# Products over 640 tokens on TensorE: column segments of 512 and 128 in place of 320 and 320

## The chip, the cores and the metric

The kernel runs on one core of a Trainium2 chip. The metric is the device time of one execution in microseconds, from the first to the last instruction with what lies around them; the median of several runs counts. The core has five engines with their own instruction queues: TensorE (PE; its weight loads are listed apart as PEld), VectorE (DVE), ScalarE (ACT), GpSimd (POOL) and SyncE (SP, which here issues most DMAs).

## The reference, cut to what matters

One layer of a hybrid diffusion backbone for 640 tokens (128 context tokens and 512 latent ones) of width 1024, in float32:

```
z = h @ w_in + b_in                      # 1024 -> 3584, h = modulated LayerNorm of x
u_a, u_b, g_a, g_b = split(z)            # 1024, 512, 1024, 1024 columns
v = gelu(s5_forward(u_a) + s5_backward(u_a))
v = v * sigmoid(v @ w_glu + b_glu)
ya = v @ w_proj_a
yb = pool_mix(u_b, w_pool, pool_scale) @ w_proj_b
x = LN(alpha*x + gate*((sigmoid(g_a)*ya + sigmoid(g_b)*yb) @ w_out + b_out))
x = LN(alpha*x + gate*(square(relu(h2 @ w_mlp1 + b_mlp1)) @ w_mlp2 + b_mlp2))
```

## The kernel before, in words

All float32 products are made of three products of the float32r type: each operand is split into a high part and a low remainder (`split`, lines 320 to 322: a cast on ACT, a subtraction on DVE), and high by high, high by low and low by high are added up in PSUM (`PASS`, line 331). The tokens lie along the columns of the moving operand, the output channels are the 128 columns of the stationary one. A PSUM bank holds 512 float32 columns, so the 640 tokens need two banks (`bank2`, a tile of 128 x 2 x 512) and two matmuls for each pass and each block of 128 input channels. `SEG` (line 31) says which tokens go to which: 0 to 319 into the first bank, 320 to 639 into the second. `mm_k` (lines 333 to 337) issues, for one block of input channels, the three passes, and in each pass the two segments with the same 128x128 weights, so the segments alternate: first segment, second segment, first, second. Each matmul has its own weight load in the trace.

Products that go through `mm_k` with `SEG`, in order of time, with the matmuls of each:

- the input projection `w_in`, 28 products of 48 matmuls: two next to the making of the operand `hk` (`chan`, line 388), six for `u_a` (`ua_evac`, each followed by two calls of `more_in`, which transpose and project on TensorE too), and 20 "fillers" for `u_b` and the gates (`plain`, `halves`), of which 16 are called during the scan, one in four of the scan's steps on DVE, and three are cut into halves between the calls of `out_proj`;
- `pool_map`, four products of 6 matmuls, and `pool_proj`, eight products of 24 matmuls, between calls of `out_proj`;
- `w_glu`, eight products of 48 (line 845, the first two interleaved at line 843), and `w_pa`, eight products of 48 (line 873).

That is 1344 + 24 + 192 + 384 + 384 = 2328 matmuls or 1164 pairs of segments. The two MLP products use `mm_k` with `SEG_MLP` (384 and 256 columns) or other loops (`mlp_first`, line 979; `prod`, line 1048; line 1119) and are not touched.

A finished pair of banks is read in one instruction: `v2(ps)` takes the first 320 columns of each bank as a 128 x 2 x 320 view, and `tv(t)` views the 640 columns in SBUF the same way. ACT reads it with a bias and a function (lines 364, 612, 629, 708, 852), or DVE multiplies it by a gate (lines 718, 874). Weights come in with `wsplit`: a DMA on SP into one of two raw buffers, the split into one of three `wh` buffers. Other TensorE work around these products is plain float32 (lines 489, 503, 557, 597, 600, 237).

Of the kernel before, what the change touches and what calls it, by code (L numbers as in the profile page):

```python
# [13 lines left out]
AF = mybir.ActivationFunctionType  # L14
# [5 lines left out]
NT = 640  # L20
NTT = 5
KT = 8
TC = 8
# [4 lines left out]
FF = 4 * D  # L28
ALPHA = 2.0 ** 0.25
EPS = 1e-6  # L30
SEG = ((0, 320), (320, 320))
SEG_MLP = ((0, 384), (384, 256))


C_BIN, C_BADA, C_BGLU, C_PSC, C_BM1, C_N = 0, 28, 76, 84, 88, 120
# [3 lines left out]
def hybrid_kernel(ctx: ExitStack, tc: tile.TileContext, xin, cc, w_ada0, w_ada, w_in, w_glu, w_pa, w_pool, w_pb,  # L39
                  w_out, w_m1, w_m2, cols, rows, brow, lam, bpk, cpk, ddg, s0, cst, invc, out, nstate):  # L40
    nc = tc.nc
    V, S, T = nc.vector, nc.scalar, nc.tensor
# [29 lines left out]
    def bank2(name="ps"):  # L72
        return pp[0].tile([P, 2, 512], F32, tag="mm", name=nm(name))

    def bank(name="ax"):
        return pp[0].tile([P, 512], F32, tag="ax", bufs=axn[0], name=nm(name))
# [3 lines left out]
    colt = keep.tile([P, C_N], F32, name="colt")  # L80
# [243 lines left out]
    def wsplit(src, n=D, to=None):  # L324
        raw = wp.tile([P, D], F32, tag="wr", bufs=2, name=nm("wr"))
        hl = wp.tile([P, 2, D], F32R, tag="wh", name=nm("wh")) if to is None else to
        dma(raw[:, 0:n], src)
        split(raw[:, 0:n], hl[:, 0, 0:n], hl[:, 1, 0:n])
        return hl
# [3 lines left out]
    def mm_k(ps, hl, xk, k, nk, segs):  # L333
        for i, (wh, xh) in enumerate(PASS):
            for n, (o, ln) in enumerate(segs):
                T.matmul(ps[:, n, 0:ln], hl[:, wh, k * P:(k + 1) * P], xk[:, xh, o:o + ln],  # L336
                         start=(k == 0 and i == 0), stop=(k == nk - 1 and i == 2))

    def mm(hl, xk, segs=SEG):
        ps = bank2()  # L340
        for k in range(len(xk)):
            mm_k(ps, hl, xk[k], k, len(xk), segs)
        return ps

    def v2(ps):
        return ps[:, :, 0:320]

    def tv(t):
        return t.rearrange("p (n c) -> p n c", n=2)

    ud = dp.tile([KT, TC, P, NC], F32, name="ud")
    urd = dp.tile([KT, TC, P, NC], F32, name="urd")
# [8 lines left out]
    def ua_evac(m, ps):  # L361

        uj = half([P, TC, NC], "uj")
        S.activation(uj[:, ::-1, :].rearrange("p j (n c) -> p j n c", n=2),
                     v2(ps).rearrange("p n (c j) -> p j n c", j=TC),
                     AF.Identity, bias=colt[:, C_BIN + m:C_BIN + m + 1])
        dma(ud[m].rearrange("j p c -> p j c"), uj)
        ur = half([P, TC, NC], "ujr")
        S.copy(ur[:, :, 0:CP], uj[:, :, CP - 1::-1])
        S.copy(ur[:, :, CP:NC], uj[:, :, NC - 1:CP - 1:-1])  # L370
        dma(urd[m].rearrange("j p c -> p j c"), ur)
# [43 lines left out]
    for q in range(4):  # L415
# [3 lines left out]
        for hl, pu in zip(hls0, (pu0, pu1)):  # L419
            for kk in (2 * q, 2 * q + 1):  # L420
                mm_k(pu, hl, hx[kk], kk, KT, SEG)
        if q < 2:
            shift_scale(q + 2)
    ang = s5_angles()
    ua_evac(0, pu0)
    ua_evac(1, pu1)
    s5_params(*ang)
    dma(dd, ddg)
# [180 lines left out]
    def plain(m, func, dst):  # L609
        ps = mm(next_w(), hx)  # L610
        g = gt([P, NT], "g")
        S.activation(tv(g), v2(ps), func, bias=colt[:, C_BIN + m:C_BIN + m + 1])  # L612
        dma(dst, g)
# [5 lines left out]
    def halves():  # L619

        while fillers:
            m, func, dst = fillers.pop(0)
            hl, ps = next_w(), bank2()
            for k in range(KT):
                mm_k(ps, hl, hx[k], k, KT, SEG)
                if k == 3:
                    yield
            g = gt([P, NT], "g")
            S.activation(tv(g), v2(ps), func, bias=colt[:, C_BIN + m:C_BIN + m + 1])
            dma(dst, g)  # L630
            yield
# [19 lines left out]
    for m in range(2, 8):  # L651
        ua_evac(m, mm(next_w(), hx))
        more_in(2, 1)
        if m == 3:
            gen_q(0)
        if m in (4, 6):
            gen_t(m // 2 - 2)
            gen_q(m // 2 - 1)
# [43 lines left out]
    def pool_map(gi, p, wph):  # L702
        ph = hslot([P, 2, NT], F32R, "ph")
        split(p, ph[:, 0, :], ph[:, 1, :])
        ps = bank2()
        mm_k(ps, wph[:, :, gi * P:(gi + 1) * P], ph, 0, 1, SEG)
        f = gt([P, NT], "yb")
        S.activation(tv(f), v2(ps), AF.Identity, scale=colt[:, C_PSC + gi:C_PSC + gi + 1])
        yb = hslot([P, 2, NT], F32R, "ybx")
        split(f, yb[:, 0, :], yb[:, 1, :])  # L710
        ybx.append(yb)
# [129 lines left out]
    for k in range(KT):  # L841
        for m in range(2):
            mm_k(gps[m], hls[m], vx[k], k, KT, SEG)
    for m in range(KT):
        ps = gps[m] if m < 2 else mm(wsplit(w_glu[m]), vx)
# [22 lines left out]
    for m in range(KT):  # L868
# [4 lines left out]
        ps = mm(wsplit(w_pa[m]), [gx[:, k] for k in range(KT)])  # L873
# [47 lines left out]
    for t in range(NTT):  # L921
        st = 0 if t else 1
        x = x1s[t]
        ps = bank2()
# [202 lines left out]
    for t in range(NTT):  # L1127
        last = t == NTT - 1
        if t == 0:
            ps2 = bank2()  # L1130
            ps = [ps2[:, 0], ps2[:, 1]]
        else:
            ps = [bank("pse")] + ([bank2()[:, 0], bank2()[:, 0]] if last else [bank("pse")])
# [12 lines left out]
        for n, (fh, o, ln) in enumerate(parts):  # L1146
            c = slice(fh * 512 + o, fh * 512 + o + ln)
# [94 lines left out]
```

## Time and profile before

| | |
|---|---|
| median of 3 runs | 1024.67 us (1021.18 to 1029.95) |
| the profiled execution's own time | 1022.42 us |
| its span, first to last instruction | 1020.5 us |
| busy: PE / PEld / DVE / ACT | 980.2 / 888.2 / 683.5 / 410.7 us |
| mean granted TensorE clock | 0.989 of full speed |

1.9 us of the profiled execution lie outside its span. In the views, a group of instructions is named by its line, engine and operation, its tiles (out<-in) and its shapes. A busy time is the union of the group's instructions; matmuls overlap in the pipeline and their ends are modelled, so the price of one matmul in a stream is read from the starts (how long until the next piece starts, over the count), not from the duration of one.

### The profile page before, as it was taken

To read this page: it belongs to the slowest core of one execution; us is meant where nothing else is said; L and a number is where in the kernel's file an instruction comes from. 1 tells how busy PE (TensorE), PEld (TensorE's weight loads), DVE (VectorE), ACT (ScalarE), POOL (GpSimd) and SP (SyncE) were. 2 spreads that over 40 slices of the span, in tenths; PEclk is the share of its full clock that TensorE was granted. 3 is DMA by queue.
4 is the path that set the end of the run, shared out by engine and by line. 5 is a ranking of instruction groups with operands and counts; after the bars stand their busy time and mean duration, and the time that the engine had idled before them with its cause. 6 is when DMAs were issued, how large, how long until landed. Compare 5 with 4: busy or idle time off the path is not lost.

```text
span 1020.5 us, 18184 instructions
## 1 busy us (share of the span) xinstructions
PE 980.2 (96%) x7464; PEld 888.2 (87%) x7464; DVE 683.5 (67%) x1192; ACT 410.7 (40%) x687; POOL 59.5 (6%) x85
## 2 busy tenths in 40 slices
PE   4999998999999899999999999999999999999997
PEld 3898887989999799999978898889988998899886
DVE  5899878979813334546659953876855784468586
ACT  5576664322135425322243453323631364126510
POOL 0000000000285002100000001000000000000000
PEclk9999999999999999999999999999999999999998
DMA  9687666866598888867640235512232123212511
GB/s 357 218 232 205 196 199 177 223 192 189 163 287 233 223 262 302 330 202 263 232 165 21 65 107 184 130 65 73 91 106 81 53 92 105 82 42 84 185 62 62
DMA packets 116986, 166.82 MB, mean 163 GB/s; under 512 B 47720, under 2 KB 80488, under 8 KB 116904
## 3 DMA queue, kind: packets, MB, share of 16 engines
q1 hardware_dynamic: 111528, 146.27, 46.2%
q0 software_dynamic: 5376, 19.40, 5.5%
q8 instruction: 58, 0.95, 0.4%
q14 instruction: 24, 0.20, 0.1%
HBM read 135.30 MB, written 30.34 MB: 162 GB/s over the span
## 4 chain that ended last, share of the span: by engine, by line
PE 74%; DVE 10%; DMA 6%; ACT 5%; issue 4%; SPq 1%; DVEq 0%; ACTq 0%; POOLq 0%
PE ps L336 26%; PE ps L1119 16%; PE ps L1048 8%; PE psx L1048 6%; PE pse L1142 3%; PE ps L928 3%; PE psy L597 2%; PE psz L503 2%; PE pst L489 2%; PE psa L237 1%; PE ps L1142 1%; DVE wh L322 1%; DMA c<-in_cpk_dram 1%; PE psy L600 1%; ACT wh L321 1%
## 5 line engine op out<-in xcount | busy, mean ns | idle before, releaser
L336 PE MATMUL ps<-hk,wh 128*128 128x320 f32 x1344 | 213.6, 316 | 6.4 <-ACT g L612 3.0
L336 PEld LDWEIGHTS ps<-hk,wh 128*128 128x128 f32 x1344 | 200.4, 191 | 13.0 <-ACT g L612 4.3
L322 DVE TENSOR_TENSOR wh<-wr,wh 128x1024 fp32r<-128x1024 f32 (+1 forms) x113 | 128.2, 1135 | 101.7 <-ACT wh L321 100.6
L321 ACT CAST wh<-wr 128x1024 fp32r<-128x1024 f32 (+1 forms) x113 | 109.2, 966 | 170.6 <-PE ps L1119 91.9
L1119 PE MATMUL ps<-wh,fx 128*128 128x512 f32 x720 | 164.2, 389 | 0.0
L1119 PEld LDWEIGHTS ps<-wh,fx 128*128 128x128 f32 x720 | 134.9, 188 | 27.8
L336 PEld LDWEIGHTS ps<-gx,wh 128*128 128x128 f32 x384 | 56.4, 187 | 3.3 <-issue 2.9
L336 PE MATMUL ps<-gx,wh 128*128 128x320 f32 x384 | 58.7, 310 | 0.0
L336 PEld LDWEIGHTS ps<-vx,wh 128*128 128x128 f32 x384 | 56.4, 188 | 2.5 <-ACT sg L852 2.1
L336 PE MATMUL ps<-vx,wh 128*128 128x320 f32 x384 | 58.1, 311 | 0.0
L1048 PE MATMUL psx<-h,wh 128*128 128x320 f32 x288 | 47.6, 308 | 0.0
L1048 PE MATMUL ps<-h,w 128*128 128x320 f32 x288 | 46.5, 307 | 0.0
L1048 PEld LDWEIGHTS psx<-h,wh 128*128 128x128 f32 x288 | 43.7, 187 | 0.2
L1048 PEld LDWEIGHTS ps<-h,w 128*128 128x128 f32 x288 | 43.2, 187 | 0.0
L612 ACT ACTIVATE g<-ps,colt 128x640 f32<-128x640 f32 x17 | 13.5, 794 | 71.4 <-PE ps L336 71.4
L890 DVE TENSOR_TENSOR ps<-ps,gate 128x512 f32<-128x512 f32 (+2 forms) x39 | 28.1, 748 | 21.1 <-PE ps L1119 16.1
L597 PE MATMUL psy<-zt,q 64*128 64x80 f32 x512 | 41.4, 273 | 0.0
L597 PEld LDWEIGHTS psy<-zt,q 64*128 64x128 f32 x512 | 35.0, 188 | 3.1 <-issue 2.9
L928 PE MATMUL ps<-wo,mx 128*128 128x512 f32 x150 | 36.6, 392 | 0.2 <-ACT wo L321 0.2
L336 PE MATMUL ps<-ybx,wh 128*128 128x320 f32 x192 | 32.5, 329 | 3.5 <-DVE gb L718 3.1
L336 PEld LDWEIGHTS ps<-ybx,wh 128*128 128x128 f32 x192 | 30.6, 203 | 4.4 <-issue 3.2
L225 POOL DMA_DIRECT2D wa<-in_w_ada_dram x32 | 16.9, 532 | 295.1 <-PE psa L237 110.3
(267 smaller groups left out, 1604.1 us busy)
## 6 DMA issues: line engine op xcount, KB each, us to landing
wr<-in_w_m_dram SPq DMA_DIRECT2D x64, 512.0 KB
wa<-in_w_ada_dram POOLq DMA_DIRECT2D x32, 512.0 KB, 5.9
wr<-in_w_in_dram SPq DMA_DIRECT2D x28, 512.0 KB
qd<-q SPq DMA_DIRECT2D x8, 1024.0 KB
q<-qd SPq DMA_DIRECT2D x16, 512.0 KB
x<-in_xin_dram SPq DMA_DIRECT2D x10, 512.0 KB
wa<-in_w_ada_dram SPq DMA_DIRECT2D x10, 512.0 KB
tm<-sd SPq DMA_DIRECT2D x8, 512.0 KB
```

The costliest lines, as they stand in the source:

```text
L225: nc.gpsimd.dma_start(w, w_ada[self.mod, :, k * D:(k + 1) * D])
L321: S.copy(hi, raw)
L322: V.tensor_tensor(lo, raw, hi.bitcast(F32), op=ALU.subtract)
L336: T.matmul(ps[:, n, 0:ln], hl[:, wh, k * P:(k + 1) * P], xk[:, xh, o:o + ln], start=(k == 0 and i == 0), stop=(k == nk - 1 and i == 2))
L489: T.transpose(ps[:, i * P:(i + 1) * P], wt[:, 2 * h + i // 2, i % 2, :], ident)
L503: T.matmul(ps[64 * d:64 * d + 64, o:o + NC], w[:, 2 * h + l, r, 64 * d:64 * d + 64], us[m][d][:, (e % 2) * 4 + 2 * h + l, :], start=True, ...
L597: T.matmul(o, q[d, l, i, :], zt[d, 0:NC // 2, i, 4 * e + l, :], start=(i == 0), stop=False, skip_group_check=True)
L890: V.tensor_tensor(ps, ps, g[:, c0:c1], op=ALU.mult)
L928: T.matmul(ps[:, n, :], mx[k][:, xh, t * P:(t + 1) * P], wo[k][:, wh, n * 512:(n + 1) * 512], start=(k == 0 and i == 0), stop=(k == KT - 1 ...
L1048: T.matmul(ps, hl[:, wh, c + k * P:c + (k + 1) * P], rq[b][:, xh, k, :], start=(start and k == 0 and i == 0), stop=(stop and k == 3 and i ...
L1119: T.matmul(pt[t], fx[k][:, xh, t * P:(t + 1) * P], hl[:, wh, kk * 512:(kk + 1) * 512], start=(k == 0 and i == 0), stop=(k == 7 and i == 2))
L1142: T.matmul(ps[n][:, 0:ln], fx[k][:, xh, t * P:(t + 1) * P], hl[:, wh, o_:o_ + ln], start=(k == 0 and i == 0), stop=(k == 7 and i == 2))
```

## The change

`SEG` becomes 512 and 128 columns: the first matmul of a pair fills its bank, the second writes the first 128 columns of the next bank. The 640 results then lie in one unbroken run over the two banks, so `v2` gives the first 640 columns of the flattened tile and `tv` gives the tile itself; the evacuation in `ua_evac` loses the same split.

```
-SEG = ((0, 320), (320, 320))
+SEG = ((0, 512), (512, 128))
...
     def v2(ps):
-        return ps[:, :, 0:320]
+        return ps.rearrange("p a b -> p (a b)")[:, 0:NT]

     def tv(t):
-        return t.rearrange("p (n c) -> p n c", n=2)
+        return t
...
-        S.activation(uj[:, ::-1, :].rearrange("p j (n c) -> p j n c", n=2),
-                     v2(ps).rearrange("p n (c j) -> p j n c", j=TC),
-                     AF.Identity, bias=colt[:, C_BIN + m:C_BIN + m + 1])
+        S.activation(uj[:, ::-1, :], v2(ps).rearrange("p (c j) -> p j c", j=TC), AF.Identity, bias=colt[:, C_BIN + m:C_BIN + m + 1])
```

The number of instructions, their order and what waits for what stay as they are.

## Rows read from the trace of the kernel before

**Rows 1.** The page: the span, busy time of each engine, granted clock in 40 slices.
```profile
span 1020.5 us, 18184 instructions
...
PE 980.2 (96%) x7464; PEld 888.2 (87%) x7464; DVE 683.5 (67%) x1192; ACT 410.7 (40%) x687; POOL 59.5 (6%) x85
...
PEclk9999999999999999999999999999999999999998
```

**Rows 2.** The page: the chain that ended last, by engine and by line.
```profile
PE 74%; DVE 10%; DMA 6%; ACT 5%; issue 4%; SPq 1%; DVEq 0%; ACTq 0%; POOLq 0%
PE ps L336 26%; PE ps L1119 16%; PE ps L1048 8%; PE psx L1048 6%; PE pse L1142 3%; PE ps L928 3%; PE psy L597 2%; PE psz L503 2%; PE pst L489 2%; PE psa L237 1%; PE ps L1142 1%; DVE wh L322 1%; DMA c<-in_cpk_dram 1%; PE psy L600 1%; ACT wh L321 1%
```

**Rows 3.** Groups by line and shape, PE: xcount | busy us, mean ns | idle before.
```profile
L336 PE MATMUL ps<-hk,wh 128*128 128x320 f32 x1344 | 213.6, 316 | 6.4 <-ACT g L612 3.0 <-DVE sq L566 1.5 <-DVE hk L404 0.8
...
L336 PE MATMUL ps<-vx,wh 128*128 128x320 f32 x384 | 58.1, 311 | 0.0
L597 PE MATMUL psy<-zt,q 64*128 64x80 f32 x512 | 41.4, 273 | 0.0
```

**Rows 4.** The chain in order of time: start us, us, what, count.
```profile
260.67 21.35 PE ps L336 x144
...
282.85 0.45 PE psy L597 x8
283.30 0.22 PE psy L600 x4
...
383.90 21.31 PE ps L336 x144
...
643.96 54.43 PE ps L1119 x240
```

**Rows 5.** Timeline of PE, 597 to 644 us: start us, us to the last end.
```profile
601.58 5.82 PE L979 MATMUL ps<-h,wh 128*128 128x256 f32 x48
607.23 2.99 PE L979 MATMUL psx<-h,wh 128*128 128x256 f32 x24
```

**Rows 6.** Groups by line and shape, PEld (weight loads).
```profile
L336 PEld LDWEIGHTS ps<-hk,wh 128*128 128x128 f32 x1344 | 200.4, 191 | 13.0 <-ACT g L612 4.3 <-issue 3.1 <-DVE hk L405 1.7
...
L503 PEld LDWEIGHTS psz<-u,w 128*64 128x64 f32 x512 | 21.7, 139 | 5.0 <-issue 4.3 <-ACT zt L508 0.5 <-ACT w L490 0.2
...
L557 PEld LDWEIGHTS psq<-q,bm 64*32 64x32 f32 x512 | 7.5, 105 | 2.0 <-issue 1.7
```

**Rows 7.** Groups by line and shape, ACT: evacuations of PSUM.
```profile
L612 ACT ACTIVATE g<-ps,colt 128x640 f32<-128x640 f32 x17 | 13.5, 794 | 71.4 <-PE ps L336 71.4
...
L962 ACT ACTIVATE fr<-ps,colt 128x384 f32<-128x384 f32 x8 | 4.7, 586 | 21.3 <-PE ps L336 20.2 <-DVE h L322 0.8 <-DVE fx L322 0.2
...
L962 ACT ACTIVATE fr<-ps,colt 128x256 f32<-128x256 f32 x5 | 2.2, 469 | 1.8 <-PE ps L979 1.8
```

**Rows 8.** Stretches: length, then busy us (xcount) of PE, PEld, DVE, ACT, POOL; clock, DMA.
```profile
50.00:165.00 115.00, 107.56 (x1274) 96.53 (x1272) 96.64 (x159) 76.05 (x191) 0.21 (x1) 0.97 0.71 200
...
196.00:260.00 64.00, 61.34 (x572) 59.60 (x570) 57.40 (x167) 17.20 (x33) 0.69 (x1) 0.97 0.63 189
...
345.00:391.00 46.00, 42.51 (x411) 40.90 (x410) 16.68 (x28) 16.37 (x22) 0.00 (x0) 0.93 0.82 244
391.00:456.00 65.00, 65.00 (x509) 59.63 (x512) 29.66 (x35) 23.36 (x28) 10.06 (x19) 1.00 0.81 279
```

**Rows 9.** The chain in order of time: pieces that are not TensorE's.
```profile
203.44 7.09 DMA wr<-in_w_in_dram
...
258.91 1.22 DVE wh L322
...
345.28 8.36 DMA gb<-gbd
...
365.86 4.04 DMA wr<-in_w_pb_dram
```

## The prediction

> **What bounds the kernel now.** I began with the page's busy times: TensorE's matmuls cover 96% of the span, its weight loads 87%, DVE 67%, and the granted clock is at its upper level, 2.4 GHz, for 90% or more of every slice but the last [rows 1]. A busy PE is not a PE at its peak, so the next view is the chain that ended last. It runs through PE for 74% of the span, and the line that the change touches, L336, is its largest part with 26% [rows 2], some 270 us. L336 also issues the 384 and 256 column matmuls of three MLP products, which stay. So a change of the price of these matmuls is paid almost in full, and the question is that price.
>
> The groups by shape give durations: 316 and 311 ns for a 320 column matmul [rows 3]. Those overlap, so prices come from starts. The chain shows unbroken streams: 144 matmuls of 320 columns in 21.35 and 21.31 us, which is **148.3 ns** each, and 240 of 512 columns in 54.43 us, **226.8 ns** each [rows 4]. In the timeline 48 matmuls of 256 columns start at 601.58 and the next group at 607.23: 5.65 us, **117.7 ns** each [rows 5]. From 256 to 512 columns the price rises by 109.1 ns, 0.426 ns per column. This line gives 145.0 ns at 320 columns, and L336 pays 3.3 more; I put that to its alternation between two banks.
>
> **What the change does, part by part.** Instruction counts, order and waits are the same. 1164 pairs of 320 and 320 become pairs of 512 and 128 columns (2328 matmuls, counted in the code; the trace has 1344 on `hk` and 384 on `vx` [rows 3]). The total of columns is the same, so on the line alone nothing would happen. What can change is the short matmul's slot.
>
> *Now*: a pair is 2 x 148.3 = 296.6 ns.
>
> *The 512 half*: 226.8 ns [rows 4], plus 3.3 for alternation.
>
> *The 128 half*: no float32r matmul below 256 columns is in this trace, so its price needs bounds. From below: the line extended, 117.7 - 128 x 0.426 = 63 ns. But each matmul brings its own weight load, and the load for the next 512 half has to run beside the 128 half. Loads of 128, 64 and 32 columns last 188 to 191, 139 and 105 ns [rows 6]: 0.86 ns for each column, so some 110 ns of a 128 column load are loading and the rest is a fixed latency that overlaps. Is there a stretch that loads pace? Yes: `out_proj` (L597, L600) alternates two row halves with 80 column matmuls and 128 column loads, and 12 records take 0.45 + 0.22 = 0.67 us [rows 4], 55.8 ns each or 112 ns for each row half. If one load is under way at a time in a row half, the full array, which uses both, pays 112 ns too. The 256 column stream is the second bound: same load, full array, 117.7 ns from start to start [rows 5]; there the load hides, so load and swap fit in 117.7. So a slot paced by the load is 112 to 118 ns. I take 117.7, the nearest row in kind (float32r, full array), plus 3.3.
>
> *From above*: the price of plain float32. The code calls L597 256 times (16 x 4 x 2 x 2) and the trace has 512 records [rows 3], two for each matmul, so such a product costs two slots of 112 ns, 223 ns.
>
> The Trainium skill, page "TensorE: Matmul & The Clock Gate", section "LDWEIGHTS (loading the stationary operand)", speaks against this change: a load takes its columns divided by 1.2 GHz, whatever the matmul behind it. For 128 columns that is an estimate of 107 ns; the 0.86 ns per column of [rows 6] agree. By this figure alone a pair would be 334 ns and the sum below 43 us in place of 63.
>
> *Sum*: a pair after is 226.8 + 117.7 + 6.6 = 351 ns, 54.5 more than now. Times 1164 pairs: **63 us** of TensorE time. With 112 and no extra for alternation it is 338.8, 42 more, 49 us.
>
> *The evacuation*: one instruction before and after. ACT reads 640 columns as two runs in 794 ns, while 256 and 384 columns as one run take 469 and 586 ns [rows 7], 0.91 per column, which gives 820 at 640. The two runs cost nothing that one run would save: 0 us, and ACT and DVE wait for these products anyway (71.4 us at L612).
>
> **What of the 63 us shows.** By stage, pairs from the code, 54.5 ns each:
> - 0 to 50 us, 48 pairs, 2.6 us. The operand is being made; I count 1.6.
> - 50 to 165, 144 pairs, 7.8 us. PE is busy 107.6 of 115 us [rows 8], DVE 96.6, and the two take turns on the chain: 5.8.
> - 165 to 282, 17 products, 408 pairs, 22.2 us. Between 196 and 260 DVE carries the chain, with a weight DMA of 7.09 us and splits on it [rows 9]. PE is busy 61.3 of these 64 us [rows 8], so it has about 3 to 5 us of slack before it is the bound again: 17.
> - 282 to 345, 84 pairs, 4.6 us: 4.4.
> - 345 to 391, 96 pairs, 5.2 us. The chain holds two DMAs of 8.36 and 4.04 us [rows 9], and 3.5 of 46 us of PE are idle [rows 8]; a slower product hides under them: 2.6.
> - 391 to 519, 384 pairs, 20.9 us. PE is busy 65.0 of 65 us [rows 8]; all 20.9.
>
> Together 52 us. Where I cost slack at something, the cover is DVE's scan and those DMAs; without the cover the full 63 would show. The profiled execution took 1022.4 us, so **1074 us**. It lay 2.3 us below the median of the runs, which are 8.8 us apart, so no correction. The load-paced case alone spans 1058 to 1088: 49 us of which three quarters show, up to the full 63.
>
> **The rivals.**
> *A, not slower: weight loads run ahead.* One mechanism: if TensorE can hold two loads in advance, the load for the next 512 half is done beside the present one, since two loads of 110 ns fit into the pair's 293. The slot is then 63 ns by the line, the pair 226.8 + 63 + 6.6 = 296.4, and the time stays at 1022. For it: 188 ns loads already overlap each other at 148 ns starts, and 55.8 ns per record in `out_proj` [rows 4] could also be read as one serial load path that needs only 56 ns for 128 columns. It decides once the slot falls below 70 ns. Against it: durations that grow with columns [rows 6], and `out_proj`, where 80 columns would stream in 34 ns by the line, or 68 at twice its slope, and yet a row half takes 112. The same page of the Trainium skill, section "Back-to-back issue gap", gives 81 ns per matmul for sustained pairs of load and 128 column matmul; with that the pair is an estimate of 308 to 314 ns and the time about 1035. No row here shows such a stream.
>
> *B, the short matmul is priced as plain float32.* 223 ns for the slot: pair 226.8 + 223 + 6.6 = 456, 160 more, 186 us, of which some 172 show: 1194. For it: below 256 columns every product in the trace is plain float32, so nothing shows that the cheap float32r rate holds there. Against it: one record per float32r matmul, and one straight line, at every width seen.
>
> *C, the load starts only when the 128 columns have streamed.* Slot 63 + 118 = 181: pair 414, 118 more, 137 us, about 122 showing: 1144. Against it: the loads at 256 columns hide fully.
>
> **How the numbers follow.** Load-paced 0.60, A 0.15 (the page's 81 ns is in it), B 0.18, C 0.07. The predicted time is that of the likeliest, 1074. From 1050 to 1205 the range holds the load-paced case with its bounds, C, and B: about 0.83. A is left out. About 1%, 10 us, is what a measurement of this kernel can tell from no change. Within that lies A: 0.13. Faster needs A with a slot well below the line: 0.02. The rest, 0.85, is slower.
>
> **What would show it.** In the profile after, L336 has two shapes, 128x512 and 128x128. In the `w_glu` and `w_pa` stages, an unbroken product of 48 matmuls takes 24 x 0.351 = 8.4 us (7.1 by A, 10.9 by B, 9.9 by C). The start of a 128 column matmul to the next start should be 112 to 121 ns. The input stage up to 165 us should grow by 7 us, 391 to 519 by 21 us, and everything after 519 us should keep its length. If `ACT g L612` gets shorter, the evacuation step is wrong. The prediction falls if the pair costs 300 ns or less, or over 400, or if the scan stage from 165 to 282 grows by less than 10 us while the pair costs what I say.

## The result, and the profile after

The changed kernel takes 1110.8 us (median), the one before 1026.7 us beside it: a ratio of 1.085, interval 1.079 to 1.091. The medians lie 84 us apart and the two profiled executions, on which the readings below go, 87 us (1109.3 and 1022.4 us), where 52 had been forecast. The time lies inside the range, but outside the range of 1058 to 1088 that was given for the load-paced case alone.

The page of the changed kernel: span, busy times, granted clock in 40 slices.

```profile
span 1107.1 us, 18215 instructions
...
PE 1035.9 (94%) x7464; PEld 896.6 (81%) x7464; DVE 685.9 (62%) x1192; ACT 409.2 (37%) x687; POOL 59.5 (5%) x85
...
PEclk9989998888999999999999999999999999999999
```

TensorE is busier by 56 us, but its share fell from 96% to 94% [rows 1]: it also stands still more. The granted clock is below 90% in the slice from 55 to 83 us and in those from 166 to 277 us; before, in the last slice alone. The instruction counts of the engines are those of before; the 31 more of the first line are not among them.

The chain of the changed kernel, some of its pieces in order of time (start us, us, what, count).

```profile
268.23 10.39 PE ps L336 x48
...
503.12 8.33 PE ps L336 x48
...
512.46 8.33 PE ps L336 x48
```

A product of 48 matmuls in the `w_glu` stage takes 8.33 us, 347 ns for a pair. The forecast was 351 ns, 8.4 us. So the price of the pair came out, and it can't be the whole story: 1164 pairs at 50.5 ns more are 59 us, even if nothing of it hides. Here are the stages, divided at the first scan step that takes the projected input (`ta<-ta,zt`), the first matmul of `out_proj`, the first of `w_glu` and the last of `w_pa`, read from the first and last starts of these tiles. The lines of the first two of these points, before and then after (count, shortest, median and longest in ns, first and last start in us):

```profile
L526 DVE TENSOR_TENSOR ta<-ta,zt x63: 279/285/425, 164.5 to 275.6; 128x128 f32<-128x128 f32 x48, 128x256 f32<-128x256 f32 x15
L597 PE MATMUL psy<-zt,q x512: 267/269/336, 282.0 to 383.4; 64*128 64x80 f32 x171
```

```profile
L524 DVE TENSOR_TENSOR ta<-ta,zt x63: 280/285/419, 182.6 to 288.1; 128x128 f32<-128x128 f32 x48, 128x256 f32<-128x256 f32 x15
L595 PE MATMUL psy<-zt,q x512: 267/270/335, 343.5 to 446.0; 64*128 64x80 f32 x171
```

| stage | before, us | after, us | grew by | forecast |
|---|---|---|---|---|
| input, to the first scan step | 164.5 | 182.6 | 18.1 | 7.4 |
| scan and its fillers, to `out_proj` | 117.5 | 160.9 | 43.4 | 17 |
| `out_proj`, pooling, to `w_glu` | 109.0 | 111.1 | 2.1 | 7.0 |
| `w_glu` and `w_pa` | 127.3 | 147.2 | 19.9 | 20.9 |
| all behind | 502.2 | 505.3 | 3.1 | 0 |

The stages after the scan came close to the forecast or below it. The excess lies in the input and the scan. There TensorE waits. The waits of PE from 160 to 345 us in the changed kernel (who waited for whom: us in total, times, longest):

```profile
PE ps L336 <- DVE sq L564: 13.0, 2, 9.5
PE ps L336 <- ACT g L610: 10.7, 1, 10.7
PE pst L487 <- DVE wt L453: 5.8, 1, 5.8
```

The waits of PE for a pair of banks before, from 150 to 285 us:

```profile
PE ps L336 <- ACT g L612: 3.0, 2, 1.8
PE ps L336 <- DVE sq L566: 1.5, 2, 0.8
```

(Lines behind 364 lie two lower after the change: L610 is the L612 of [rows 7].) The timeline of PE and of ACT around the wait for ACT shows what happens (start us, us to the last end, [idle before <-releaser]):

```profile
209.67 1.16 PE L555 MATMUL psq<-q,bm 64*32 64x128 f32 x64
221.51 27.81 PE L336 MATMUL ps<-hk,wh 128*128 128x512 f32 x144 [10.68 <-ACT g L610]
...
218.70 0.31 ACT L740 COPY last<-zt 128x128 f32<-128x128 f32 x1 [15.35 <-DVE zt L525]
219.04 0.31 ACT L742 COPY zt<-s0t 128x128 f32<-128x128 f32 x1
219.37 1.28 ACT L610 ACT_TABLE_LOAD   x1
220.66 0.79 ACT L610 ACTIVATE g<-ps,colt 128x640 f32<-128x640 f32 x1
```

ACT holds a copy of the scan's state (L740) that waits 15.35 us for DVE's scan. The evacuation (the reading of a finished product out of PSUM) of a product that TensorE has long finished stands behind it in ACT's queue, and TensorE, which has only two pairs of banks, waits for that evacuation. In the built queue of the kernel before, this copy stands behind six evacuations by the line L612; after the change it stands behind four. **The order within the queues is not the same**: this kernel's queues are ordered by the layer that builds it (the builder, further down), and the new segment sizes made that layer write a new order for all five engines. In the built queues, 967 of 6312 places on PE, 524 of 1192 on DVE, 193 of 676 on ACT, 125 of 374 on SP and 23 of 81 on POOL hold another instruction. With segments of 320 and 320 and the evacuation as one run, the order that the layer writes is the one of before in every place; so it is the segment sizes that change it.

The new order lets TensorE do less during the scan. In DVE's queue an addition that frees a pair of banks (L566 before, L564 after) stands, during the scan, behind 2, 12, 24 and 34 scan steps before and behind 4, 23, 48 and 63 after, and between the first and the last scan step DVE splits 12 weights before and 8 after. So the scan itself ends early (its last step starts at 288 us, 106 us after its first; before 111 us), and TensorE still has fillers until 343.5 us, 55 us later; before it was 6 us.

### The profile page after: what moved, and what is told of

It is laid out like the page before. It is cut to its first block, busy times and chain, and to the rows that moved or that the text cites. A ratio compares the mean times of both kernels' runs of the same rounds, so it can differ in the third digit from the quotient of the medians.

```text
span 1107.1 us, 18215 instructions
## 1 busy us (share of the span) xinstructions
PE 1035.9 (94%) x7464; PEld 896.6 (81%) x7464; DVE 685.9 (62%) x1192; ACT 409.2 (37%) x687; POOL 59.5 (5%) x85
## 4 chain that ended last, share of the span: by engine, by line
PE 68%; DVE 12%; DMA 10%; issue 4%; ACT 4%; SPq 1%; POOL 0%; DVEq 0%; ACTq 0%; POOLq 0%
PE ps L336 24%; PE ps L1117 15%; PE ps L1046 8%; PE psx L1046 6%; PE ps L926 4%; PE pse L1140 3%; DMA wa<-in_w_ada_dram 3%; DMA c<-in_cpk_dram 2%; DMA yn<-yd 2%; PE psy L595 2%; DVE zt L525 2%; PE psz L501 2%; DVE ta L522 2%; DVE wh L322 1%; DVE ta L524 1%
## 5 line engine op out<-in xcount | busy, mean ns | idle before, releaser
L336 PE MATMUL ps<-hk,wh 128*128 128x512 f32 x1344 | 249.8, 343 | 27.0 <-DVE sq L564 13.0
L336 PEld LDWEIGHTS ps<-hk,wh 128*128 128x128 f32 x1344 | 208.3, 196 | 60.6 <-issue 14.5
L336 PE MATMUL ps<-gx,wh 128*128 128x512 f32 (+1 forms) x384 | 67.3, 333 | 0.0
L336 PE MATMUL ps<-vx,wh 128*128 128x512 f32 (+1 forms) x384 | 66.9, 334 | 0.0
L336 PEld LDWEIGHTS ps<-gx,wh 128*128 128x128 f32 x384 | 57.3, 189 | 11.0 <-issue 2.9
L336 PEld LDWEIGHTS ps<-vx,wh 128*128 128x128 f32 x384 | 57.5, 189 | 10.2 <-ACT sg L850 2.1
L610 ACT ACTIVATE g<-ps,colt 128x640 f32<-128x640 f32 x17 | 13.5, 796 | 115.8 <-PE ps L336 115.8
L926 PEld LDWEIGHTS ps<-wo,mx 128*128 128x128 f32 x150 | 27.7, 188 | 10.1 <-ACT wo L321 3.0
L336 PE MATMUL ps<-ybx,wh 128*128 128x512 f32 x192 | 34.4, 335 | 0.1
```

The source lines that it names most:

```text
L926: T.matmul(ps[:, n, :], mx[k][:, xh, t * P:(t + 1) * P], wo[k][:, wh, n * 512:(n + 1) * 512], start=(k == 0 and i == 0), stop=(k == KT - 1 ...
```

## The experiments

The order can be kept apart from the segment sizes: instructions have the same numbers in both kernels, so the order of one can be written out and imposed on the other, engine by engine.

```
+def _pin(tc, nc):
...
+            if prev is not None:
+                tc.add_manual_dep(traced[name], prev, info, reason="pinned order")
+            prev = name
...
         hybrid_kernel(tc, *args)
+        _pin(tc, nc)
```

**1. The changed segments in the old order.** Edit: the changed kernel, with every queue in the order of the kernel before.

> The changed kernel (512 and 128 columns) with every engine's queue issued in the order that the kernel before has. Theory 1 (price and order): a pair costs 347 ns in place of 296.6, 59 us of TensorE time, of which some 50 show, and the other 30 us of the change come from the new queue order; so this run takes about 1075 us (1065 to 1085), and the scan stage has no TensorE stall of 10 us. Theory 2 (price alone: a slower TensorE upsets the overlap of the scan whatever the order): about 1110 us.

Measured: 1061.2 us, ratio 1.036 (1.030 to 1.042). Theory 1, and 4 us below the range that it gave.

**2. The old segments in the new order.** Edit: the same lines added to the kernel before, with the order of the changed kernel written out.

> The kernel before (320 and 320 columns, two runs of 320 in the evacuation) with every engine's queue issued in the order that the changed kernel has. Theory 1: the order alone costs 20 to 40 us, 1045 to 1065 us, with TensorE standing still in the scan stage behind DVE's scan steps. Theory 2: about 1025 us, no change.

Measured: 1073.5 us, ratio 1.048 (1.042 to 1.055). The order alone costs 4.8%, somewhat more than expected; the segments alone cost 3.6%. The sum, 8.4%, is the change's 8.5%. Theory 2 is out. The input stage shows it in PE's waits for `wt`, first after the change (20 to 183 us), then in run 1 (20 to 172 us): with the old order 7.8 us of them go.

```profile
PE pst L487 <- DVE wt L453: 13.0, 2, 7.2
```

```profile
PE pst L487 <- DVE wt L453: 5.2, 2, 3.5
```

The timeline of PE in run 2, in the scan:

```profile
203.92 1.16 PE L557 MATMUL psq<-q,bm 64*32 64x128 f32 x64
219.90 22.69 PE L336 MATMUL ps<-hk,wh 128*128 128x320 f32 x144 [14.83 <-ACT g L612]
```

With the old, faster segments TensorE meets the same wait at the same place, and it is longer, 14.83 us: TensorE arrives earlier (its products before end sooner), the scan step on which the copy waits does not. In run 1 the five stages take 171.6, 128.7, 110.2, 144.8 and 502.3 us, so they grew by 7.1, 11.2, 1.2, 17.5 and 0.1.

Stretches of the scan after the change and, in the second fence, in run 1 (length, then busy us of PE, PEld, DVE, ACT, POOL; granted clock, DMA share, GB/s):

```profile
209.00:222.00 13.00, 2.32 (x71) 1.82 (x70) 12.33 (x36) 3.24 (x5) 0.00 (x0) 0.71 0.55 150
222.00:250.00 28.00, 28.00 (x198) 24.33 (x205) 24.08 (x75) 5.80 (x12) 0.00 (x0) 0.89 0.42 124
250.00:275.00 25.00, 15.49 (x105) 13.20 (x91) 24.00 (x75) 4.11 (x10) 0.00 (x0) 0.80 0.29 86
```

```profile
200.00:225.00 25.00, 25.00 (x206) 21.84 (x205) 21.59 (x60) 6.50 (x12) 0.00 (x0) 1.00 0.64 195
225.00:250.00 25.00, 25.00 (x207) 21.77 (x205) 24.10 (x66) 5.98 (x16) 0.00 (x0) 1.00 0.51 162
250.00:275.00 25.00, 25.00 (x206) 21.79 (x205) 22.52 (x80) 5.69 (x8) 0.69 (x1) 1.00 0.55 167
```

With the old order PE has no gap and the clock is granted in full. With the new one, each of the two waits of about 10 us is followed by matmuls at the lower level, 1.2 GHz: the granted clock is 0.50 from 221.5 to 227.5 us and 1.00 again from 229.5 us on, and 0.50 from 268.2 to 272.0 us and 1.00 again from 274.0 us on. The product that starts at 268.23, behind a wait of 9.5 us, takes 10.39 us where the others take 8.33. So such a stall costs some 2 us more than it lasts.

**3. Is the short slot paced by the weight load?** Edit: segments of 448 and 192, the first at the end of its bank so that the 640 stay one run; old order.

```
-SEG = ((0, 512), (512, 128))
+SEG = ((0, 448), (448, 192))
+LEAD = 512 - SEG[0][1]
...
-                T.matmul(ps[:, n, 0:ln], hl[:, wh, k * P:(k + 1) * P], xk[:, xh, o:o + ln],
+                c0 = LEAD if segs is SEG and n == 0 else 0
+                T.matmul(ps[:, n, c0:c0 + ln], hl[:, wh, k * P:(k + 1) * P], xk[:, xh, o:o + ln],
...
-        return ps.rearrange("p a b -> p (a b)")[:, 0:NT]
+        return ps.rearrange("p a b -> p (a b)")[:, LEAD:LEAD + NT]
```

> Segments of 448 and 192 columns in one run of 640, queues in the order of the kernel before. A slot paced by the weight load does not depend on its columns below 256: the 448 half costs 200 ns by the line, the 192 half 118 as at 256, a pair about 323 with the alternation, 26 more than now, 31 us, of which 26 show: about 1051 us. If the price follows the columns alone: a pair of 297 and about 1025 us. If every float32r matmul below 256 columns is priced as plain float32, two loads of 112 ns: a pair of 430 and about 1165 us.

Measured: 1037.2 us, ratio 1.012 (1.008 to 1.016). That lies between the load-paced forecast and the linear one, so the time alone doesn't decide; the unbroken streams do. The chain at the start of `w_glu`, first of run 3 (where L336 has become L338), then of run 1:

```profile
386.62 22.73 PE ps L338 x144
```

```profile
402.34 24.64 PE ps L336 x144
```

72 pairs take 22.73 us with 448 and 192, 315.7 ns a pair, and 24.64 us with 512 and 128, 342.2 ns. Take the long half off by the line (226.8 ns measured at 512; 199.5 ns at 448 is an estimate between the widths of [rows 4] and [rows 5]): what the short half adds is 116.2 ns at 192 columns and 115.4 ns at 128. A third fewer columns change it by less than 1 ns; at 256 a matmul cost 117.7 [rows 5]. That is a floor, and the price by columns (90 and 63 ns) and plain float32's 223 ns are both out. In the timeline of weight loads of run 1, with narrow windows, one sees the pace (start us, us to the last end, count):

```profile
450.16 0.19 PEld L336 LDWEIGHTS ps<-vx,wh 128*128 128x128 f32 x1
...
450.16 0.30 PEld L336 LDWEIGHTS ps<-vx,wh 128*128 128x128 f32 x2
...
450.50 0.19 PEld L336 LDWEIGHTS ps<-vx,wh 128*128 128x128 f32 x1
...
450.50 0.30 PEld L336 LDWEIGHTS ps<-vx,wh 128*128 128x128 f32 x2
```

Two loads start 0.11 us apart (the two together last 0.30 us, one 0.19), then nothing starts for 0.23 us, and the pattern repeats every 0.34 us, the pair. 0.11 us is what the durations by columns had given for a load [rows 6]. By the rule of the Trainium skill, page "TensorE: Matmul & The Clock Gate", section "LDWEIGHTS (loading the stationary operand)", columns over 1.2 GHz, a load of 128 columns takes an estimate of 107 ns; the 0.11 us between two loads agree. The Trainium skill's 81 ns for each 128 column matmul (same page, section "Back-to-back issue gap") are not met here: with them the pair would be an estimate of 308 ns, and 342.2 ns were measured.

The starts of the matmuls put the extra time in another place than the prediction did. The same run, windows of 10 ns from 450.48, 450.49 and 450.55 us on:

```profile
450.21 0.44 PE L336 MATMUL ps<-vx,wh 128*128 128x512 f32 x1
450.21 0.50 PE L336 MATMUL ps<-vx,wh 128*128 128x512 f32 x2
450.21 0.78 PE L336 MATMUL ps<-vx,wh 128*128 128x512 f32 x3
```

A piece grows by a matmul in the window in which that one starts: the 128 column matmul starts 0.28 us after the 512 column one, and the next 512 column matmul only 0.06 us after that, again 0.34 us for the pair. So from a short start to the next the record has 60 ns, near the 63 of the line, and not 112 to 121; the 54 ns that are missing stand in front of the short matmul. In run 3 the two distances are 0.09 us, by the line too, and 0.23 us. The price of the pair is shown, and that its extra does not depend on the columns of the short half; that the weight load makes it is read from the 0.11 us between loads. No run changed the loads alone, so this cause is argued, not shown by an experiment.

**4. The evacuation as one run, alone.** Edit: as in 3, with other sizes; old order, which is also the order that the builder gives it.

```
-SEG = ((0, 448), (448, 192))
+SEG = ((0, 320), (320, 320))
```

> The evacuation alone: segments stay 320 and 320, but the first lies at the end of its bank, so that the 640 results are one unbroken run and are read as such; queues in the order of the kernel before. All theories: within 1% of the kernel before, and the 640 column evacuation on ACT stays at 794 ns (within 20).

Measured: 1023.2 us, ratio 1.001 (0.997 to 1.004), and the group of evacuations on ACT is the same (this run's L338 is L336 in the kernel before):

```profile
L612 ACT ACTIVATE g<-ps,colt 128x640 f32<-128x640 f32 x17 | 13.5, 795 | 71.0 <-PE ps L338 71.0
```

795 ns against 794 [rows 7]. The one run brings nothing, and imposing an order that the layer would write anyway costs nothing by itself.

**5. Does one misplaced wait cost?** Edit: the changed kernel and its own order, but the two copies on ACT (L740, L742) are moved behind the next evacuation, its weight split and the copies behind it. ACT's queue by lines:

```
 L610 L321
-L740 L742
 L610 L321 L560 L561 L537 L538 L537 L538
+L740 L742
 L610 L321
```

> The changed kernel with its own queue order but for two copies on ACT: the copy of the scan's state (L740) and the one behind it (L742), for which ACT waited 15.4 us with a finished evacuation queued behind them, stand behind that evacuation and the copies of the next product. Theory 1a (each misplaced wait costs for itself): TensorE's stall of 10.7 us goes, about 1100 us. Theory 1b (the order as a whole runs TensorE ahead of DVE; DVE's addition at L564 stands behind the same scan steps and frees the next bank pair): the stall comes back one product later, the time falls by 3 us or less, about 1108 to 1111 us.

Measured: 1118.1 us, ratio 1.093 (1.089 to 1.097), against 1.085 (1.079 to 1.091) for the change: not better, rather 7 us worse. The scan stage is as long as after the change (162.0 us against 160.9 in the profiled executions); what made the other stages longer is not known. The wait of 10.7 us is gone, and PE waits elsewhere (waits of PE from 180 to 340 us):

```profile
PE ps L336 <- DVE sq L564: 18.3, 3, 14.3
PE ps L336 <- DVE wh L322: 4.2, 1, 4.2
PE ps L336 <- ACT g L610: 1.0, 1, 1.0
```

So 1a falls and 1b holds in kind: DVE's addition at L564 stands behind the same scan steps and frees the banks no sooner. The wait on ACT was only the first of several that come from one cause.

**6. Whose order?** Edit: the changed kernel with only DVE's queue in the old order; the builder orders the others around it.

```
-    for steps in json.loads(zlib.decompress(base64.b64decode(_ORDER))).values():
+    for steps in [json.loads(zlib.decompress(base64.b64decode(_ORDER)))["DVE"]]:
```

> The changed kernel with only DVE's queue in the order of the kernel before; the builder orders the other engines around it. In the changed kernel the additions at L564 that free a pair of banks stand behind 4, 23, 48 and 63 scan steps, before behind 2, 12, 24 and 34. If DVE's order is what costs: most of the 50 us go, 1065 to 1080 us, and TensorE's waits for L564 vanish. If it is the order of TensorE, ACT or the DMAs: 1095 us or more.

Measured: 1077.8 us, ratio 1.054 (1.049 to 1.058). 33 of the 50 us between the change and run 1 are gone, and no wait of PE is left in the scan, which is 124.8 us long (run 1: 128.7). Of the remaining 17 us, 14 are in the input stage, which still ends at 185.6 us (run 1: 171.6); there PE waits for DVE's operands of the state projection. The stage of `out_proj` is 4.8 us longer than in run 1, `w_glu` and `w_pa` 2.5. The waits of PE from 20 to 186 us in this run:

```profile
PE pst L487 <- DVE wt L453: 14.7, 5, 5.9
```

Since the other queues differ here from those of both kernels, whose order makes this rest is open.

**7. Is it the alternation of banks that separates 148 ns from the line?** Edit, on the kernel before, in the old order:

```
-        for i, (wh, xh) in enumerate(PASS):
-            for n, (o, ln) in enumerate(segs):
+        for n, (o, ln) in enumerate(segs):
+            for i, (wh, xh) in enumerate(PASS):
```

> The kernel before with the two loops of mm_k exchanged: three passes into the first bank, then three into the second; queue order as before. If the alternation of two banks costs the 3.3 ns that separate 148.3 ns from the line, 2328 of them are 7.7 us: about 1016 us, and an unbroken stream takes 145 to 147 ns for each matmul. If not: no change, 1023 us.

Measured: 1025.7 us, ratio 1.002 (1.000 to 1.005): no gain. The bank now changes at every third matmul in place of every one, and the stream at the start of `w_glu` is what it was [rows 4]:

```profile
387.31 21.31 PE ps L336 x144
```

With two thirds of the changes gone, none of the 3.3 ns went, so they are not the alternation's. What they are stays open.

**8. The price without any imposed order.** Edit: 512 and 128 only for `w_glu` and `w_pa`, whose evacuations read one run; all queues keep the old order up to the `w_glu` stage by themselves.

```
+SEG_L = ((0, 512), (512, 128))
...
-        ps = gps[m] if m < 2 else mm(wsplit(w_glu[m]), vx)
+        ps = gps[m] if m < 2 else mm(wsplit(w_glu[m]), vx, SEG_L)
...
-        ps = mm(wsplit(w_pa[m]), [gx[:, k] for k in range(KT)])
+        ps = mm(wsplit(w_pa[m]), [gx[:, k] for k in range(KT)], SEG_L)
```

> 512 and 128 columns only in the w_glu and w_pa products (384 of the 1164 pairs, all after the scan), everything before as in the kernel before; no order is imposed, and every queue has the old order up to the w_glu stage. If what is lost to the new order is lost in the input and scan stages, only the price is left: 384 x 45.7 ns = 17.5 us, about 1041 us. If the new order costs in the later stages too: 1050 us or more.

Measured: 1046.8 us, ratio 1.020 (1.015 to 1.026), 21 us with an interval of 16 to 26; the price alone gives 17.5. Agreed, within that interval: in the profiled execution, from the first start of `w_glu` to the last of `w_pa` are 145.0 us against 127.3 before, 17.7 more. Behind the scan, the price shows in full and the order adds little or nothing.

None of these versions is faster than the kernel before.

## Why the prediction was right, and where it was wrong

*The direction and the price of the short half were right, and the mechanism fits.* The likeliest case was a slot of 112 to 118 ns, set by the weight load; in runs 1 and 3 the short half adds 115 to 116 ns to the pair at 128 and at 192 columns, near the 0.11 us between two loads. The pairs that rivals A (the load runs ahead, 296 ns, or 308 to 314), B (priced as plain float32, 456 ns) and C (414 ns) gave are out: run 1 measured 342.2. Where the slot lies was wrong, see run 3: the records have it in front of the short matmul.

*The size of the pair's term was off.* The forecast was 54.5 ns more for each pair; run 1 against [rows 4] gives 342.2 - 296.5 = 45.7 ns. Of the 8.8 ns between them, 6.6 are the 3.3 ns that I had put to the alternation of banks and had added to both halves of the new pair: run 7 shows that the alternation costs nothing, and the new pair has no such surcharge (226.8 + 117.7 = 344.5 is above the measured 342.2 already). The other 2.3 are 115.4 in place of 117.7. The sum is then 1164 x 45.7 = 53 us, not 63.

*What hides was off too.* Run 1 grew by 37 us of these 53. By stage (pairs x 45.7): input 8.8, of which 7.1 show; scan 18.6, of which 11.2; `out_proj` and pooling 8.2, of which 1.2; `w_glu` and `w_pa` 17.5, of which all. In the `out_proj` stage almost all of the share is hidden, where I had let 7 of 10 us through. Before, PE waits there once for 3.1 us for DVE's reading of a product (`gb`, L718), which waits for the first DMA of [rows 9], and the granted clock is 0.59 from 352 to 358 us and 0.88 from there to 366; in run 1 that wait is gone and the clock of the stage is 1.00. By an estimate from these clocks the second is worth some 3 us more; I had counted the cover of the DMAs too low and had no term for the clock. In the scan stage PE's idle time fell from 4.5 us to 1.1; that is 3.3 of the 7.4 us hidden, and what hid the rest is not shown.

*The step that failed* is the first sentence of the part on what the change does: "Instruction counts, order and waits are the same." The section on the change, ahead of the prediction, says the same. The counts are; the order is not, and it carries 50 us of the change, more than half (run 2: 4.8%; the change less run 1: 1110.8 - 1061.2). I read the kernel's loops as the order of its queues, and no rival had a new order in it. With the old order the forecast of 1074 would have been 13 us too high (run 1: 1061); with the new one it was 37 too low. That the time fell inside the range is luck: the range reached above 1088 only for rivals C and B, and neither has anything to do with it.

*What the order does* is shown by runs 2, 5 and 6: it puts the scan on DVE first and TensorE's fillers late, and a TensorE that is faster than this order allows for stands still behind scan steps, first at one wait, and when that is taken away, at the next. Why the builder wrote it so is only argued: an order with 8 weight splits in place of 12 during the scan would fit an estimate of the short matmul far above its 115 ns. The runs don't show that estimate.

*What was named as a sign* came out so: pair 347 ns in the `w_glu` stage (8.33 us against 8.4), 391 to 519 us longer by 20 against 21, the tail longer by 3 against 0, the evacuation unchanged. One sign did not come: from the start of a 128 column matmul to the next start, 112 to 121 ns were named and the record has 60 (run 3), though the pair costs what was said. None of the three conditions under which the prediction was to fall came true, and none of them would have caught a new order. The input stage (18 against 7) and the scan stage (43 against 17) were the signs that something else was at work.

## What to carry to other kernels

In these runs a matmul that streams in less time than its own weight load takes saved nothing by being shorter: with 128 weight columns in float32r a pair cost its long half plus 115 ns, with 192 columns in the short half as with 128. So 640 tokens are better cut into 320 and 320 than into 512 and 128: the columns that the long half takes over are paid there, and below 256 the short half gives nothing back for them. Where a layer orders the queues, any change of a shape can reorder all engines; compare the built queues before pricing anything, and separate the two effects by running the new shapes in the old order and the old shapes in the new one. A single long wait in such an order may be a symptom: removing it here only moved the stall to other waits.

## What the runs showed of the hardware that I had not expected

With a load of 128 weight columns for each, the price of a float32r matmul at full clock lies on a line between 512 and 256 columns (226.8 and 117.7 ns), and the short half of a pair adds 116.2 ns at 192 columns and 115.4 ns at 128, where the line would give 90 and 63. The records of the starts show these as 60 ns behind the start of the 128 column matmul and 281 behind that of the 512 column one. At 320 columns it is 148.0 ns, 3 above the line, whether the bank changes at each matmul or at every third. Behind a wait of TensorE of 9.5 us the granted clock was 0.50 (from 268.2 to 272.0 us after the change), and the product there took 2 us more than the others.
